# A head's normalisation and gating beside the opening of the next head, and a reordered start, in a hybrid decoder layer on one core

## The chip, the cores and the metric

The kernel runs on one core of a Trainium2 chip. The metric is device time in microseconds (us) of one execution. The engines are TensorE (PE in the profile, its weight loads PEld), VectorE (DVE), ScalarE (ACT), GpSimd (POOL) and SyncE (SP, which here only issues DMAs). A number such as L555 is a line of the kernel before.

## The reference

One layer, sequence 1024, width 2048, everything in fp32. A wide projection makes 15 column blocks of 512; four token mixers work on them (A, a gated convolution; B, a gated recurrence with 4 heads; C, differential attention with 4 heads; D, a chunked spatial gate); every mixer's output is multiplied by the silu of its own gate block; then an output projection, a layer norm and a gated addition of a second input.

```
h = x @ w_in                                   # (1024, 2048) @ (2048, 7680)
a_b,a_c,a_x, b_q,b_f,b_i, c_q,c_k,c_v, d_u,d_v, g_a,g_b,g_c,g_d = split(h, 15)
y_a = a_b * conv3(a_c * a_x)
# B, per head:  S_t = diag(f_t) S_{t-1} + (1-f_t) i_t^T ;  o_t = S_t^T q_t ;  rms norm
# C, per head:  (softmax(q1 k1) - lam * softmax(q2 k2)) v ;  rms norm
y_d = gelu(d_u) * (tril(W_s) LN(gelu(d_v)) + b)
y = concat(y_a*silu(g_a), y_b*silu(g_b), y_c*silu(g_c), y_d*silu(g_d)) @ w_out
x = layer_norm(ALPHA * x + y)
x = x + (p @ w_pe) * sigmoid(x @ w_pg)
```

## The kernel before

**The large products.** Each fp32 operand is split into a high part (a cast on ACT, L139) and the rest (a subtraction on DVE, L140), both in a reduced fp32 form; a product is then three runs of 128x512 matmuls (high by high, high by rest, rest by high), 24 matmuls in all for one 1024-long sum. The 2x2 block products of the input projection are done with seven products in place of eight (names P1, P6, P7, P4 in the first pass over 30 pairs of column blocks, N1, N4, A12 in the second). Sums of weight blocks (L262 to L271) and of x blocks (L312 to L320) are made on DVE. The first pass leaves its results in DRAM (`stash`), the second pass adds to them, and when a pair is complete its blocks are kept in DRAM (`h`) or, for gates, put through a silu and kept in `g_dram`.

**What runs beside the second pass.** Mixer work is written as Python generators, one for each head: `unit_c` and `mix_c` for a head of C, `unit_b` and `mix_b` for one of B, `values_d`, `norm_d` and `unit_d` for D. A completed pair appends its generator to `queue`. `step()` runs the first generator of the queue to its next `yield`; the second pass calls it after every second of the eight parts of a product, that is after every six matmuls. So the number of yields sets how many matmuls stand on PE between two pieces of mixer work. A head goes so: it issues the loads of its blocks from `h` (`back`, on POOL's queue), waits some yields, works, and ends with `rms` (a scale, a power on POOL, and the multiplication L548), seven yields, and `finish`: eight transposes on PE (`yt`, L555), two multiplications by the gate on DVE (L557), and a store to `y_dram` (L558, on SP's queue). Only then does the next generator begin, and the first thing that it does is to issue its loads.

**What sets the order.** Each engine takes its instructions in one order that a scheduler fixes when the kernel is built; work within `early()` is moved ahead of what stands before it in the code. Buffers are tiles with tags; a tag has one buffer unless the text says otherwise (`raw` 6, `wh` and `wl` 2 each, `E` 2, `pp` and `mx` 4 PSUM banks each). Work that writes a tile waits until the last user of the same buffer is done. So an engine that waits for a buffer or a load holds up what stands behind it, and `wh`, which PE needs for the next product, is often what stands behind it on ACT.

**The beginning.** SP loads one 512 KB block after another. `small_setup` (L98) makes small constants with some tiny DVE operations and one exponential on ACT (L103). The first pass then does P1 of pairs 0 to 3, P6 of pair 0, and so on, with the x sums S2 and S3 made in between.

**The end of the mixers.** After the last pair the loop `while len(queue) > 1: step()` and then the first output product (`tk`, L437) run the rest of the queue; the last head, B3, is in that product.

Of the kernel before, what the change touches and what calls it, by code (L numbers as in the profile page):

```python
# [16 lines left out]
P = 128  # L17
# [21 lines left out]
def trunk_kernel(  # L39
# [58 lines left out]
    def small_setup(pool):  # L98
        nc.gpsimd.dma_start(ident, tri[:, 0, :])
        nc.gpsimd.dma_start(chan_sb, chan)  # L100
        V.tensor_copy(lb_max, lb_raw)
        V.tensor_tensor(lb_e, lb_raw, lb_max, op=ALU.subtract)
        S.activation(lb_e, lb_e, AF.Exp)  # L103
        V.tensor_copy(one_lb, lb_e)
        V.reciprocal(one_lb, one_lb)
        V.tensor_tensor(lb_e, lb_e, one_lb, op=ALU.mult)
        V.tensor_copy(lb, lb_e)
        V.tensor_tensor(lb, lb, lb_e, op=ALU.subtract)
        V.tensor_scalar(one_lb, lb, -1.0, 1.0, op0=ALU.mult, op1=ALU.add)
        V.tensor_scalar_mul(da_g, chan_sb[:, 20:24], 1.0 - LAM_INIT)  # L110
        lamw = pool.tile([P, 4, 64], F32, tag="sm", bufs=4, name="lamw")
        nc.gpsimd.dma_start(lamw, lam_in.broadcast_to([P, 4, 64]))
        lamp = pool.tile([P, 2, 64], F32, tag="sm", bufs=4, name="lamp")
        V.tensor_tensor(lamp, lamw[:, 0::2, :], lamw[:, 1::2, :], op=ALU.mult)
        V.tensor_reduce(lamt[:, 0:2], lamp, axis=AX.X, op=ALU.add)
        S.activation(lamt[:, 2:4], lamt[:, 0:2], AF.Exp)
        V.tensor_tensor(lamt[:, 5:6], lamt[:, 3:4], lamt[:, 2:3], op=ALU.subtract)
        V.tensor_scalar_add(neg_lam, lamt[:, 5:6], -LAM_INIT)

    queue = []

    def step():
        while queue:
            if next(queue[0], queue) is not queue:
                return
            queue.pop(0)

    def drain():  # L130
        while queue:
            step()

    early = lambda: tc.high_priority(offset=4000)
# [70 lines left out]
    with tc.tile_pool(name="first", bufs=1) as first:  # L205
# [69 lines left out]
        def first_product(what, g, w=None):  # L275
            w = w or first_w(what, g)
            if what == "P1":
                chain[g] = pp.tile([P, H], F32, tag="pp", name=f"a{g}")
            ps = chain[g]
            products(ps, w, xs[{"P1": "A11", "P6": "S2", "P7": "S3", "P4": "A22"}[what]], what == "P1", True)  # L280
            if what in ("P1", "P7"):
                evs[g] = epool.tile([P, 2, H], F32, tag="e", name=f"ev{g}")

            S.copy(evs[g][:, {"P1": 0, "P6": 1, "P7": 1, "P4": 0}[what], :], ps)
            if what in ("P6", "P4"):
                i = 0 if what == "P6" else 1
                nc.scalar.dma_start(stash[g][:, i : i + 3 : 2, :], evs[g])
# [7 lines left out]
        for w in ("A11", "S2", "S3"):  # L295
            xs[w] = tuple([xa(f"{w}{i}{g}") for g in range(2)] for i in "hl")
        split_x = lambda w, t, q: split(t, pair(xs[w][0], q), pair(xs[w][1], q))
        with early():
            for q in range(4):
                nc.sync.dma_start(pair(r11, q), x_blk(1, 1, q))  # L300
                split_x("A11", pair(r11, q), q)
                if q == 0:
                    w_first = first_w("P1", 0)
        first_product("P1", 0, w_first)
        for g in (1, 2, 3):
            first_product("P1", g)
        with early():
            for q in range(4):
                nc.sync.dma_start(pair(r21, q), x_blk(2, 1, q))
                r22.append(sm(f"r22{q}"))  # L310
                nc.sync.dma_start(r22[q], x_blk(2, 2, q))
                V.tensor_tensor(pair(r21, q), pair(r21, q), r22[q], op=ALU.subtract)  # L312
                V.tensor_tensor(pair(r21, q), pair(r21, q), pair(r11, q), op=ALU.subtract)
                split_x("S2", pair(r21, q), q)
        for g in (2, 3):
            b[g].pop("11")
        first_product("P6", 0)
        with early():
            for q in range(4):
# [9 lines left out]
                split_x("A22", r22[q], q)  # L329
        first_product("P7", 1)  # L330
        first_product("P4", 0)
        first_product("P6", 2)
        first_product("P4", 1)
        first_product("P6", 3)
        first_product("P7", 2)
        first_product("P1", 4)
        first_product("P4", 2)
        first_product("P7", 3)
        first_product("P6", 4)
        first_product("P4", 3)  # L340
        small_setup(first)
        queue.extend([x_sums(q) for q in range(4)] + [w_sums(*HALVES[0], kk) for kk in range(8)])
        for g in range(5, NG):
            first_product("P1", g)
            step()
            if g == NG - 1:
                x_build("N1")
            first_product("P7", g - 1)
            first_product("P6", g)
            if g == NG - 1:  # L350
                x_build("A12")
            first_product("P4", g - 1)
# [112 lines left out]
    with tc.tile_pool(name="work", bufs=1) as work:  # L465
# [125 lines left out]
        def unit_b(j):  # L591
            k, f, qt, lw = wt("k1"), back(B_F, j, wt("l1")), back(B_Q, j, wt("q1")), wtE()
            iv = back(B_I, j, wtE())
            for _ in range(4):
                yield
            S.activation(k, f, AF.Sigmoid, scale=-1.0)
            S.activation(f, f, AF.Sigmoid)
            S.activation(k, k, AF.Copy, scale=one_lb[:, j : j + 1])
            V.tensor_scalar(f, f, one_lb[:, j : j + 1], lb[:, j : j + 1], op0=ALU.mult, op1=ALU.add)
            V.tensor_scalar_max(lw, f, SPLIT)  # L600
            V.tensor_scalar(f, f, F_FLOOR, SPLIT, op0=ALU.max, op1=ALU.min)
            S.activation(lw, lw, AF.Ln)
            S.activation(f, f, AF.Ln, scale=1.0 / SPLIT)
            V.tensor_tensor(f, f, lw, op=ALU.add)
            yield
            vtok = turned(wt("vt"), iv)
            yield
            yield from mix_b(j, k, f, qt, vtok)

        def mix_b(j, kt, lt, qt, vtok):  # L610
            at = ch(wt("a1"))
            G.memset(at, 0.0)

            near = wt("near", (P, 8, 32))
            G.memset(near, 0.0)

# [59 lines left out]
            pair_ = factors(LEVELS[0])  # L676
            yield
            yield
            for li, m in enumerate(LEVELS):
                ahead = factors(LEVELS[li + 1]) if li + 1 < len(LEVELS) else None  # L680
                yield
                gram(li, m, *pair_)
                pair_ = ahead
                if li + 1 < len(LEVELS):
                    yield
                    yield
# [8 lines left out]
            yield  # L695
            ktok = ch(wtV())
            transpose_to(ktok, ch(kt))
            o = ch(wtE())
            yield
            state = None  # L700
            ss = small.tile([P, 8], F32, tag="ss", name="ss")
            for b in range(2):
# [25 lines left out]
                S.copy(o[:, 4 * b : 4 * b + 4, :], pso)  # L728
                for c in range(4):
                    square(ss, 4 * b + c, pso[:, c, :])  # L730
            gt = gate_back("v1", 4 + j)
            rms(o, ss)
            for _ in range(7):
                yield
            finish(o, hg_g(j), gt, wt("o"), 4 + j)

        def unit_c(j):
            kraw, vraw, qraw = back(C_K, j, wt("o")), back(C_V, j, wtE()), back(C_Q, j, wtE())  # L740
            for _ in range(4):
                yield
            kh = [wt(t, dt=F32R) for t in ("l1", "q1")]
            kl = [wt(t, dt=F32R) for t in ("k1", "v1")]
            for mp in range(2):
                own = slice(64 * mp, 64 * mp + 64)
                oth = slice(64 - 64 * mp, 128 - 64 * mp)
                src, hi = kraw[own, :], kh[mp][own, :]
                S.copy(hi, src)
                S.copy(kh[mp][oth, :], src)  # L750
                V.tensor_tensor(kl[mp][own, :], src, hi.bitcast(F32), op=ALU.subtract)
                S.copy(kl[mp][oth, :], kl[mp][own, :].bitcast(F32))
            yield
            vtok = turned(wt("vt"), vraw)
            yield
            qs = [wt(t, dt=F32R) for t in ("a1", "x1")]
            for mp in range(2):
                own = slice(64 * mp, 64 * mp + 64)
                oth = slice(64 - 64 * mp, 128 - 64 * mp)
                src, hi = qraw[own, :], qs[mp][own, :]  # L760
                S.copy(hi, src)
                V.tensor_tensor(qs[mp][oth, :], src, hi.bitcast(F32), op=ALU.subtract)
            yield
            yield
            yield
            yield from mix_c(j, kh, kl, qs, vtok)

        def mix_c(j, kh, kl, qs, vtok):
# [58 lines left out]
            for i in range(NCH):  # L827
# [6 lines left out]
                last = (i, turn(i, a_t), rc)  # L834
                if i >= 4:
                    yield
            yield
            values(*last)
            gt = gate_back("l1", j)
            rms(o, ss)  # L840
            for _ in range(7):
                yield
            finish(o, da_g[:, j : j + 1], gt, gt, 8 + j)

        vd = []

# [401 lines left out]
```

## Time and profile before

| | before |
|---|---|
| median of 3 runs | 2127.43 us (2127.39 to 2134.34) |
| the profiled execution | 2130.79 us, span 2129.0 us |
| mean granted TensorE clock | 0.985 of full speed |
| PE busy | 2034.2 us, 96% of the span |
| DVE busy | 1358.8 us, 64% |
| ACT busy | 876.6 us, 41% |
| POOL busy | 150.1 us, 7% |
| DMA | 443.69 MB, 208 GB/s over the span |

PE is busy nearly always, so the time is close to the sum of its matmuls; what is not matmul is in the waits of PE, each of which has a line in the views of waits and of the timeline (idle time in square brackets, with what ended it). A wait of PE that is long can also be followed by a stretch in which the granted clock is half: the column PEclk of a stretch tells it (1.00 is 2.4 GHz throughout, a mean below it says what part of the stretch was at 1.2 GHz).

### The profile page before, as it was taken

What the parts mean: (1) busy time and instruction counts of PE and PEld (TensorE: products, weight loads), DVE (VectorE), ACT (ScalarE), POOL (GpSimd) and SP (SyncE); (2) the same over time, 40 slices, a digit from 0 to 9 for tenths busy, and PEclk for the clock granted to TensorE, in tenths of its full rate; (3) what the DMA queues carried; (4) which work ended last, traced back from release to release, by engine and by line L of the source; (5) the groups of instructions that cost most, each with busy time, mean ns of one, the idle gap of its engine ahead of it and who ended that gap; (6) DMA issues with size and microseconds to landing.
All of it is one profiled execution on the core that took longest, in us unless ns stands there. A gap on an engine that the chain in (4) does not pass through costs nothing. (4 is left out here: it accounts for less than half of the span.)

```text
span 2129.0 us, 27564 instructions
## 1 busy us (share of the span) xinstructions
PE 2034.2 (96%) x10732; PEld 1659.9 (78%) x10732; DVE 1358.8 (64%) x1679; ACT 876.6 (41%) x1304; POOL 150.1 (7%) x228
## 2 busy tenths in 40 slices
PE   7999999999999989999899999998999999999989
PEld 5788888778787777778678778777878888888867
DVE  7644545545455445557557678786767999355785
ACT  4322222222223446662665556563222345433432
POOL 0000001101100000010000000000121100000000
PEclk8999999999999999999999999999999999999999
DMA  6756767767768755467554554687687643423563
GB/s 238 240 192 225 261 230 251 278 241 248 268 236 287 257 170 177 130 208 250 181 165 135 197 190 159 209 309 245 231 300 254 223 168 119 138 92 107 191 200 133
DMA packets 169763, 443.69 MB, mean 208 GB/s; under 512 B 14432, under 2 KB 14704, under 8 KB 168352
## 3 DMA queue, kind: packets, MB, share of 16 engines
q1 hardware_dynamic: 120928, 292.80, 42.1%
q0 software_dynamic: 28064, 101.93, 13.4%
q10 hardware_dynamic: 20640, 47.19, 5.7%
q8 instruction: 84, 1.38, 0.3%
q14 instruction: 47, 0.39, 0.1%
HBM read 310.80 MB, written 131.07 MB: 208 GB/s over the span
## 5 line engine op out<-in xcount | busy, mean ns | idle before, releaser
L139 ACT CAST wh<-b 128x1024 fp32r<-128x1024 f32 x180 | 189.0, 1051 | 520.5 <-PE a L188 351.8
L437 PE MATMUL tk<-th,ah 128*128 128x512 f32 x832 | 326.8, 396 | 4.9 <-ACT ah L139 2.3
L437 PE MATMUL tk<-th,al 128*128 128x512 f32 x832 | 325.4, 391 | 5.2 <-DVE al L140 5.2
L437 PE MATMUL tk<-tl,ah 128*128 128x512 f32 x832 | 321.7, 392 | 2.3 <-DVE tl L140 2.3
L140 DVE TENSOR_TENSOR wl<-b,wh 128x1024 fp32r<-128x1024 f32 x180 | 219.9, 1222 | 161.5 <-ACT wh L139 161.2
L437 PEld LDWEIGHTS tk<-th,al 128*128 128x128 f32 x832 | 156.8, 188 | 39.3 <-DVE al L140 7.8
L437 PEld LDWEIGHTS tk<-th,ah 128*128 128x128 f32 x832 | 156.4, 188 | 39.7 <-ACT ah L139 3.7
L437 PEld LDWEIGHTS tk<-tl,ah 128*128 128x128 f32 x832 | 156.4, 188 | 36.5 <-DVE tl L140 3.8
L139 ACT CAST th<-t 128x1024 fp32r<-128x1024 f32 x64 | 67.4, 1054 | 201.3 <-PE tk L437 180.1
L262 DVE TENSOR_TENSOR b<-b,b 128x1024 f32<-128x1024 f32 x30 | 36.8, 1225 | 160.1 <-DMA b<-in_w_in_dram 160.1
L140 DVE TENSOR_TENSOR tl<-t,th 128x1024 fp32r<-128x1024 f32 x64 | 78.0, 1223 | 56.9 <-ACT th L139 56.7
L188 PE MATMUL a<-A22h,wl 128*128 128x512 f32 x240 | 95.4, 398 | 10.2 <-DVE wl L140 10.2
L188 PE MATMUL b<-N1h,wh 128*128 128x512 f32 x240 | 96.9, 404 | 7.2 <-ACT wh L139 7.2
L188 PE MATMUL a<-S2h,wh 128*128 128x512 f32 x240 | 95.8, 399 | 8.3 <-ACT wh L139 5.3
L139 ACT CAST th<-b 128x1024 fp32r<-128x1024 f32 x48 | 50.5, 1052 | 125.8 <-PE tk L437 98.9
L188 PE MATMUL a<-S2h,wl 128*128 128x512 f32 x240 | 95.8, 399 | 3.6 <-DVE wl L140 3.6
L188 PE MATMUL c<-A12h,wh 128*128 128x512 f32 x240 | 97.1, 404 | 2.1 <-ACT wh L139 2.1
L188 PE MATMUL a<-S2l,wh 128*128 128x512 f32 x240 | 95.5, 398 | 3.4 <-DVE S2l L140 3.4
L188 PE MATMUL b<-N4h,wh 128*128 128x512 f32 x240 | 96.8, 403 | 0.6 <-ACT th L139 0.6
L188 PE MATMUL b<-N4h,wl 128*128 128x512 f32 x240 | 97.0, 404 | 0.0
L188 PE MATMUL b<-N1h,wl 128*128 128x512 f32 x240 | 95.8, 399 | 1.0 <-DVE wl L140 1.0
L188 PE MATMUL c<-A12h,wl 128*128 128x512 f32 x240 | 96.2, 401 | 0.5 <-DVE wl L140 0.5
(334 smaller groups left out, 4547.0 us busy)
## 6 DMA issues: line engine op xcount, KB each, us to landing
b<-in_w_in_dram SPq DMA_DIRECT2D x182, 512.0 KB, 4.7
stash<-ev ACTq DMA_DIRECT2D x60, 512.0 KB, 4.2
e<-stash SPq DMA_DIRECT2D x60, 512.0 KB, 4.9
s<-in_w_out_dram POOLq DMA_DIRECT2D x32, 512.0 KB, 7.4
ot<-s POOLq DMA_DIRECT2D x32, 512.0 KB, 5.9
h<-e SPq DMA_DIRECT2D x32, 512.0 KB, 4.9
t<-ot SPq DMA_DIRECT2D x32, 512.0 KB, 4.7
t<-b ACTq DMA_DIRECT2D x30, 512.0 KB, 4.1
```

What stands on the lines that cost most here:

```text
L139: S.copy(hi, raw)
L140: V.tensor_tensor(lo, raw, hi.bitcast(F32), op=ALU.subtract)
L188: T.matmul(ps, lhsT=w_[:, c], rhs=x_[k // 4][:, k % 4, :], start=(start and k == 0 and i3 == 0), stop=(k == 7 and i3 == 2), skip_group_che ...
L262: V.tensor_tensor(b22, b22, b12, op=ALU.add)
L437: T.matmul(ps[nn][m], lhsT=l[:, kk % 2, t], rhs=w[:, wi, :], start=(not cont and kk == 0 and i3 == 0), stop=(kk == 7 and i3 == 2), skip_gr ...
```

## The change

There are three parts. First, the ends of heads. `finish` is no longer part of the generator: it goes on a list `later`, and `step()` runs it when it has been called eight times more, while the queue goes on with the next head. `open_next()` lets the next head issue its loads before the present one is done. For this some tiles move: the gate is read back into `W` in place of `l1` or `v1` and the product is written over it; the output of a B head lies in `o` in place of `E`; the keys of a C head are loaded into `a1` in place of `o`, and its queries ahead of its values. Second, some yields are added: in `unit_c` the opening has 5 in place of 4, 3 stand between the query split and the value transposes and 4 behind these; in `unit_b` 5 in place of 4, and one more ahead of the first `gram`. Third, the beginning: SP's loads are written in the order in which they are used, five P1 products stand ahead of P6 of pair 0 in place of four (the fifth accumulates in a bank of `mx`), the list of products up to pair 5 is written out anew, and the tiny operations of `small_setup` are held behind those products, not at the start.

```diff
 def small_setup(pool):
     ...
-        V.tensor_copy(lb_max, lb_raw)
+        tc.keep_in_program_order(V.tensor_copy(lb_max, lb_raw))
     ...
-        V.tensor_scalar_mul(da_g, chan_sb[:, 20:24], 1.0 - LAM_INIT)
+        tc.keep_in_program_order(V.tensor_scalar_mul(da_g, chan_sb[:, 20:24], 1.0 - LAM_INIT))
...
-    queue = []
+    queue, later = [], []
     def step():
+        for todo in list(later):
+            todo[0] -= 1
+            if todo[0] == 0:
+                later.remove(todo)
+                todo[1]()
         while queue:
...
+    def open_next():
+        if len(queue) > 1:
+            next(queue[1])
     def drain():
-        while queue:
+        while queue or later:
             step()
...
+                pool, tag = (mx, "mx") if g == LEAD - 1 else (pp, "pp")
+                chain[g] = pool.tile([P, H], F32, tag=tag, name=f"a{g}")
...
+        LEAD = 5
+        with early():
+            load_x = lambda t, r, c, q: nc.sync.dma_start(t, x_blk(r, c, q))
+            for q in range(4):
+                load_x(pair(r11, q), 1, 1, q)
+                if q == 0:
+                    b[0] = {"11": w_raw(0, 1, 1)}
+                    w_first = w_split(b[0]["11"])
+                split_x("A11", pair(r11, q), q)
+            b[1] = {"11": w_raw(1, 1, 1)}
+            r22.extend(sm(f"r22{q}") for q in range(4))
+            for q in range(4):
+                load_x(pair(r21, q), 2, 1, q)
+                load_x(r22[q], 2, 2, q)
+                if q == 1:
+                    b[2] = {"11": w_raw(2, 1, 1)}
+            for g in range(3, LEAD):
+                b[g] = {"11": w_raw(g, 1, 1)}
+        first_product("P1", 0, w_first)
+        for g in range(1, LEAD):
+            with early():
+                w = w_split(b[g]["11"])
+                if g > 1:
+                    b[g].pop("11")
+            first_product("P1", g, w)
...
-        first_product("P6", 2)
     ...
-        first_product("P4", 3)
+        queue.extend([x_sums(q) for q in range(4)] + [w_sums(*HALVES[0], kk) for kk in range(8)])
+        for what, g in (
+            ("P6", 2), ("P4", 1), ("P6", 3), ("P7", 2), ("P6", 4), ("P4", 2),
+            ("P7", 3), ("P1", 5), ("P4", 3), ("P7", 4), ("P6", 5), ("P4", 4),
+        ):
+            first_product(what, g)
+            if what == "P1":
+                step()
...
 def unit_b(j):
-            for _ in range(4):
+            for _ in range(5):
...
 def mix_b(j, kt, lt, qt, vtok):
+            turns[0] = 0
     ...
             pair_ = factors(LEVELS[0])
             yield
             yield
+            yield
     ...
-            o = ch(wtE())
+            o = ch(wt("o"))
     ...
-            gt = gate_back("v1", 4 + j)
+            open_next()
+            gt = gate_back("W", 4 + j)
             rms(o, ss)
-            for _ in range(7):
-                yield
-            finish(o, hg_g(j), gt, wt("o"), 4 + j)
+            later.append([8, lambda: finish(o, hg_g(j), gt, gt, 4 + j)])
...
 def unit_c(j):
-            kraw, vraw, qraw = back(C_K, j, wt("o")), back(C_V, j, wtE()), back(C_Q, j, wtE())
-            for _ in range(4):
+            kraw, qraw, vraw = back(C_K, j, wt("a1")), back(C_Q, j, wtE()), back(C_V, j, wtE())
+            for _ in range(5):
                 yield
...
-            vtok = turned(wt("vt"), vraw)
-            yield
             qs = [wt(t, dt=F32R) for t in ("a1", "x1")]
...
-            yield
-            yield
-            yield
+            for _ in range(3):
+                yield
+            vtok = turned(wt("vt"), vraw)
+            for _ in range(4):
+                yield
...
 def mix_c(j, kh, kl, qs, vtok):
...
+            open_next()
             yield
             values(*last)
-            gt = gate_back("l1", j)
+            gt = gate_back("W", j)
             rms(o, ss)
-            for _ in range(7):
-                yield
-            finish(o, da_g[:, j : j + 1], gt, gt, 8 + j)
+            later.append([8, lambda: finish(o, da_g[:, j : j + 1], gt, gt, 8 + j)])
```

**The start, on ACT.** These are ACT's first rows (A11h and S2h are casts of x, wh of a weight block, ev a copy of a finished product out of PSUM, t_0 the DMA that stores a sum of weight blocks), before:

```order
L103 ACTIVATE lbt<-lbt 128x4
L139 CAST wh<-b_0_461 128x1024
L139 CAST A11h_446<-r_442 128x1024 x2
L139 CAST A11h_447<-r_443 128x1024 x2
L139 CAST wh<-b_1_503 128x1024
L139 CAST wh<-b_2_536 128x1024
L284 COPY ev_501<-a_476 128x512
L139 CAST wh<-b_3_569 128x1024
```

and now:

```order
L151 CAST A11h_446<-r_442 128x1024
L151 CAST wh<-b_0_459 128x1024
L151 CAST A11h_446<-r_442 128x1024
L151 CAST A11h_447<-r_443 128x1024 x2
L151 CAST wh<-b_1_476 128x1024
L297 COPY ev_521<-a_496 128x512
L151 CAST S2h_450<-r_444 128x1024
L297 COPY ev_552<-a_527 128x512
L151 CAST wh<-b_2_486 128x1024
```

The exponential is gone from the head of the queue and the first cast of x leads; the weight cast for the third product, which stood ahead of every copy, stands behind the copies of the first two products and a cast of S2.

**From the first C head to the second, on PE.** `yt` are the transposes of the first head's end, `tr` the value transposes and `sc` the first scores of the second head; the rows between are the matmuls of the large products. Before:

```order
L188 MATMUL c_6072<-A12h_4676,wl 128x512
L555 MATMUL yt<-ident,o 128x128 x8
L535 MATMUL tr<-ident,E 128x128 x8
L188 MATMUL c_6072<-A12h_4676,wh 128x512
...
L188 MATMUL b_5889<-N4l_4758,wh 128x512
L783 MATMUL sc<-l_5872,a_5921 128x128
L783 MATMUL sc<-q_5873,x_5922 128x128
L188 MATMUL b_5889<-N4h_4756,wl 128x512
```

and now:

```order
L200 MATMUL c_6074<-A12h_4678,wh 128x512
L578 MATMUL yt<-ident,o 128x128 x8
L558 MATMUL tr<-ident,E 128x128 x8
L807 MATMUL sc<-l_5843,a_5861 128x128
L808 MATMUL sc<-k_5845,a_5861 128x128
L810 MATMUL sc<-causal,own 128x128
L807 MATMUL sc<-q_5844,x_5862 128x128
```

Before, 35 matmuls of the large products stood between `tr` and the first `sc`; now there are none, while `yt` itself stands 7 such matmuls later.

**The last head of B, on PE.** `hgo` is the last matmul of the head that waits for its state, `yt` its end, `tk` the output product. Before:

```order
L727 MATMUL hgo<-state,q_10886 128x128 x4
L437 MATMUL tk_11271<-th,ah 128x512
L437 MATMUL tk_11271<-th,al 128x512
L437 MATMUL tk_11271<-tl,ah 128x512
...
L437 MATMUL tk_11274<-tl,ah 128x512
L555 MATMUL yt<-ident,E 128x128 x8
```

and now:

```order
L460 MATMUL tk_11239<-th,ah 128x512
L460 MATMUL tk_11239<-th,al 128x512
L460 MATMUL tk_11239<-tl,ah 128x512
L752 MATMUL hgo<-state,q_10885 128x128 x4
L578 MATMUL yt<-ident,o 128x128 x8
L460 MATMUL tk_11623<-th,ah 128x512
```

The twelve `tk` matmuls that stood between `hgo` and `yt` now stand ahead of `hgo`.

## Rows read from the trace of the kernel before

**Rows 1.** The page, first part: busy us, share of the span and instructions by engine.

```profile
PE 2034.2 (96%) x10732; PEld 1659.9 (78%) x10732; DVE 1358.8 (64%) x1679; ACT 876.6 (41%) x1304; POOL 150.1 (7%) x228
```

**Rows 2.** Stretches: length, busy (instructions) of PE, PEld, DVE, ACT, POOL; PEclk, DMA share, GB/s.

```profile
4.00:18.00 14.00, 11.42 (x87) 9.74 (x86) 8.21 (x15) 5.88 (x7) 0.00 (x0) 0.88 1.04 386
42.00:60.00 18.00, 9.94 (x24) 6.45 (x25) 18.00 (x17) 9.06 (x10) 0.00 (x0) 0.62 0.33 111
106.00:373.00 267.00, 267.00 (x1180) 221.12 (x1179) 136.06 (x117) 75.21 (x98) 21.99 (x34) 1.00 0.69 232
848.00:874.00 26.00, 20.11 (x80) 16.29 (x79) 12.14 (x18) 13.74 (x17) 0.59 (x1) 0.80 0.48 142
1015.00:1030.00 15.00, 8.91 (x30) 6.56 (x29) 9.08 (x15) 11.56 (x16) 0.00 (x0) 0.66 0.51 170
1091.00:1110.00 19.00, 14.50 (x73) 11.27 (x72) 11.97 (x15) 12.87 (x14) 1.69 (x2) 1.00 0.47 141
1260.00:1268.00 8.00, 5.37 (x26) 4.41 (x25) 5.46 (x7) 4.35 (x6) 1.65 (x1) 0.79 0.83 267
```

**Rows 3.** PE timeline, first pass: start, length, instruction, [idle before <-releaser].

```profile
7.62 1.19 PE L89 MATMUL ps_idle<-idle 128*128 128x128 bf16 x15
...
10.28 0.50 PE L188 MATMUL a<-A11h,wh 128*128 128x512 f32 x1 [1.47 <-ACT A11h L139]
...
53.91 0.79 PE L188 MATMUL a<-S2h,wh 128*128 128x512 f32 x1 [5.33 <-ACT wh L139]
```

**Rows 4.** PE timeline, second pass and the last head, at its longer waits.

```profile
756.34 0.80 PE L188 MATMUL b<-N1h,wh 128*128 128x512 f32 x1 [4.35 <-ACT wh L139]
...
850.88 0.33 PE L555 MATMUL yt<-ident,o 128*128 128x128 f32 x1 [2.25 <-DVE o L548]
...
866.09 0.47 PE L783 MATMUL sc<-l,a 128*128 128x128 f32 x1 [3.63 <-ACT l L750]
...
945.83 0.33 PE L857 MATMUL tr<-ident,E 128*128 128x128 f32 x1 [4.27 <-DVE l L557]
...
1018.41 0.66 PE L188 MATMUL c<-A12h,wh 128*128 128x512 f32 x1 [1.79 <-ACT wh L139]
...
1023.80 0.45 PE L783 MATMUL sc<-l,a 128*128 128x128 f32 x1 [4.30 <-DVE a L762]
...
1104.87 0.33 PE L783 MATMUL sc<-l,a 128*128 128x128 f32 x1 [2.86 <-ACT l L750]
...
1456.76 0.30 PE L555 MATMUL yt<-ident,E 128*128 128x128 f32 x1 [2.69 <-DVE E L548]
```

**Rows 5.** ACT timeline, same columns.

```profile
8.14 0.21 ACT L103 ACTIVATE lbt<-lbt 128x4 f32<-128x4 f32 x1 [5.91 <-DVE lbt L102]
...
753.10 1.04 ACT L761 CAST a<-E 64x1024 fp32r<-64x1024 f32 x1 [11.13 <-DMA E<-h]
...
1013.03 1.05 ACT L749 CAST l<-o 64x1024 fp32r<-64x1024 f32 x1 [7.30 <-DMA o<-h]
...
1451.34 0.59 ACT L728 COPY E<-hgo 128x512 f32<-128x512 f32 x1 [1.28 <-PE hgo L727]
```

**Rows 6.** DVE timeline, same columns.

```profile
944.41 0.69 DVE L871 TENSOR_TENSOR vt<-vt,tri 128x512 f32<-128x512 f32 x1 [4.88 <-DMA vt<-in_sg_wT_dram]
```

**Rows 7.** DMA issues: queue, count, KB each, median us from issue to landing.

```profile
b<-in_w_in_dram SPq DMA_DIRECT2D x182, 512.0 KB, 4.7
...
t<-b ACTq DMA_DIRECT2D x30, 512.0 KB, 4.1
...
y_dram<-l SPq DMA_DIRECT2D x4, 512.0 KB, 5.0
```

**Rows 8.** Waits of PE summed: line, releaser, total us, times, longest us.

```profile
PE yt L555 <- DVE E L548: 5.7, 3, 2.7
...
PE yt L555 <- DVE o L548: 5.7, 4, 2.3
...
PE gram L639 <- DVE v L664: 3.3, 3, 1.4
```

More of the change, by code (lines that the diff above doesn't have):

```diff
@@ L277, in first_product @@
             if what == "P1":
-                chain[g] = pp.tile([P, H], F32, tag="pp", name=f"a{g}")
+                pool, tag = (mx, "mx") if g == LEAD - 1 else (pp, "pp")
+                chain[g] = pool.tile([P, H], F32, tag=tag, name=f"a{g}")
             ps = chain[g]
@@ L297, in trunk_kernel @@
         split_x = lambda w, t, q: split(t, pair(xs[w][0], q), pair(xs[w][1], q))
+        LEAD = 5
[23 more added lines that the diff above has]
+            first_product("P1", g, w)
         with early():
             for q in range(4):
[L300 to L311, printed above, removed]
                 V.tensor_tensor(pair(r21, q), pair(r21, q), r22[q], op=ALU.subtract)
@@ L314, in trunk_kernel @@
                 split_x("S2", pair(r21, q), q)
-        for g in (2, 3):
-            b[g].pop("11")
         first_product("P6", 0)
@@ L331, in trunk_kernel @@
         first_product("P4", 0)
-        first_product("P6", 2)
[L333 to L339, printed above, removed]
-        first_product("P4", 3)
+        queue.extend([x_sums(q) for q in range(4)] + [w_sums(*HALVES[0], kk) for kk in range(8)])
[6 more added lines that the diff above has]
+                step()
         small_setup(first)
-        queue.extend([x_sums(q) for q in range(4)] + [w_sums(*HALVES[0], kk) for kk in range(8)])
-        for g in range(5, NG):
+        for g in range(LEAD + 1, NG):
             first_product("P1", g)
```

## The prediction, made before the changed kernel was run

> **What bounds the kernel now.** First the page's busy times: PE is busy for 96% of the span, every other engine far less [rows 1], so only what shortens PE's waits, or raises its clock, shortens the time. Then the stretches: in 106 to 373 us PE is busy throughout at full clock, 1180 matmuls in 267 us, 0.226 us each, with DVE half idle [rows 2]; there is nothing to gain there. A product of 24 matmuls takes 5.43 us by it, and a step of the queue (six matmuls) 1.36 us. Last the waits of PE, in order of time. Those that the change can touch lie at the start [rows 3], and where one head ends and the next opens [rows 4, 8]. A wait costs more than itself where the clock falls behind it: 848 to 874 us has a granted clock of 0.80 and 20.11 us of PE work, so some 0.20 x 20.11 = 4.0 us went to matmuls at 1.2 GHz; 1015 to 1030 gives 0.34 x 8.91 = 3.0 us in the same way, 42 to 60 gives 0.38 x 9.94 = 3.8, 1260 to 1268 gives 0.21 x 5.37 = 1.1, while 1091 to 1110, with waits too, shows 1.00 [rows 2]. These figures are estimates, since a mean clock says nothing of which part of the stretch was idle.
>
> The sum is made against the profiled execution, 2130.79 us (span 2129.0 and 1.79 around it). The median of the runs is 3.4 us below that, 0.16%.
>
> **The start.** Before, ACT's queue is held until 8.14 us by the exponential of the small constants, which waits for DVE [rows 5]; A11h stands behind it, and the first product begins at 10.28, 1.47 us after the idle matmuls have ended [rows 3]. With the exponential gone and x ahead, the cast of the first x block follows its load, and I place the first product right behind the idle matmuls, at 7.62 + 1.19 = 8.8 us. But that is not what the stage ends on. Loads come at 386 GB/s from 4 to 18 us [rows 2], 1.36 us for 512 KB, and DVE is busy for all of 42 to 60 us [rows 2]; PE then stands 5.33 us until 53.91 for the `wh` of P6 of pair 1 [rows 3]. In the new order that `wh` needs pair 1's block 22, whose raw buffer is free when the sum t_0 has been stored (about 36.9 us when ACT comes to it, 4.1 for the store), then 4.7 us for the load [rows 7], so 45.7, and then its sums and the split behind other DVE work of 1.2 us an operation: 53 to 54 us, as before. What changes is that a fifth P1 has been done by then. One product is 5.4 us; the new waits that I see, for the weights of the third and fourth P1 (their casts stand behind copies of finished products on ACT, as the order ahead shows for the third), lie in time that PE would otherwise spend idle before P6 of pair 1. So 5.4, less 0.4 for the load slots that P6 of pair 4 now waits for: **-5.0**. Bounds: if the chain to that `wh` also shortens by the 3 us of a new wait no longer needed, -8; if it comes a product later and another stretch like 42 to 60 (3.8 us) falls in, +3.
>
> The page "DMA: Bandwidth & Descriptors" of the Trainium skill gives under Specifications about 358 GB/s as what the memory yields to one core; the trace shows 386 over 14 us, so the measurement decides. By the page each of some twelve loads would come 0.1 us later than before's spacing says, and P6 of pair 1 would start about 1 us later.
>
> The small DVE operations moved behind the first products cost nothing: DVE is busy for 136 of 267 us where they now stand [rows 2]. Without that cover they would be twelve operations at the 0.21 us of their exponential [rows 5], 2.5 us.
>
> **First to second C head.** The wait of 2.25 us for the end's multiplication and that of 3.63 us for the split of the keys [rows 4], with 4.0 us of clock: 9.9 us. The next head's loads are issued before the first head's last values, its keys are split while the norm is computed, and the two waits fall together, since `yt`, `tr` and `sc` stand in one place on PE with seven more matmuls ahead (7 x 0.226 = 1.6 us). What is late next is that same multiplication, still behind the query split on DVE: 2.25 - 1.6 = 0.6 us, and about 1.9 for the scores' first values. 9.9 - 2.5: **-7.4**. Ends: -9.9 if nothing remains, -2 if all the operands arrive as late as before and only the clock gains.
>
> **Second C head to D.** PE stood 4.27 us because the gate product L557 was late on DVE [rows 4], behind L871, which itself waited 4.88 us for a load [rows 6]. `finish` now stands ahead of that row. But the transposes of D's first block now come right behind the head's last values, and need a load that was only just issued; I leave 1.3 us for it: **-3.0** (ends -4.3 and 0).
>
> **The opening of the third C head.** ACT waits 7.30 us for the keys, which are loaded into `o`, late, since the D branch's `o` is in use [rows 5]; behind it stand `wh` for a large product (1.79 us on PE) and the queries, for which PE waits 4.30 more [rows 4]; with the clock's 3.0 that is 9.1. With the keys in `a1`, the queries second and seven steps in place of three ahead of the scores (4 x 1.36 = 5.4 us more), 4.30 is covered and most of the rest; 2 us are left: **-7.1** (ends -9.1 and -3).
>
> **Third to fourth C head, fourth to the first of B.** The one had 2.86 us for the scores [rows 4] and, with the transposes' part of the 5.7 us in four waits [rows 8], about 4.4; the other about 1.5. By the first boundary's rule a half goes: **-3.5** together (ends -6 and 0).
>
> **B's heads.** The ends waited 5.7 us in three places, 2.69 of it at the last head, so 3.0 here, the grams 3.3 [rows 8], the clock 1.1. One more step ahead of the grams is 1.36 us, against 1.4 for the longest gram wait; the ends' squares and norm have the next head's opening beside them. **-4.0** (ends -7.4 and 0).
>
> **The last head** has no next one to stand beside. The order shows the twelve `tk` matmuls now ahead of the last `hgo`. From the copy of `hgo` at 1451.34 [rows 5] to `yt` at 1456.76 [rows 4] are 5.4 us, of which 2.69 were idle and the rest was those twelve. The wait becomes 5.4, 2.7 more, and behind a wait of about that length at 53.91 the clock is low [rows 2, 3]; a third of that 3.8 is 1.3. **+4.0** (ends +2.7 and +6.5).
>
> **The gate tile.** `finish` now writes its result over the gate in `W` and stores it: 5.0 us [rows 7] until the next head can use `W`, which C needs for its first transposed probabilities and B for its second factors. From `yt` the store lands 1.6 + 5.0 = 6.6 us later; the next head's first use stands about 22 matmuls behind, 5 us and some scores. So it is nearly even: 0.4 us at each of seven changes, **+3.0** (ends 0 and the rival below). Behind that copy on ACT stands the next `wh`.
>
> Sum: -5.0 -7.4 -3.0 -7.1 -3.5 -4.0 +4.0 +3.0 = -23.0, and 2130.79 - 23.0 = 2107.8; as the median stands a little lower, I say **2107 us**.
>
> **The rivals.**
>
> *The store of W decides* (slower). If an ACT copy waits for `W`, all that is behind it waits. What such a wait makes of PE is seen where ACT stood until 753.10 for a load and PE then waited 4.35 us for `wh` [rows 4, 5]. At that price in all seven changes, and 1.1 us of clock each as at 1260 [rows 2], it takes 7 x 5.4 = 38 us in place of the 3.0 in the sum: 2107 + 35 = 2142. It needs more than 3.7 us at each change ((23.0 + 3.0) / 7) to make the kernel slower than the profiled execution. For it: 6.6 us against 5. Against it: `wh` has two buffers, so a large product of 5.4 us is covered, and for B the user is DVE, behind which less hangs. The Trainium skill, "TensorE: Matmul & The Clock Gate", under "Wait — 56ns, not 53.3ns?", says that ACT and DVE work strictly first in, first out; the row at 753.10 agrees, and by that rule this rival stands or falls with the store alone.
>
> *The waits only move.* The loads into `E` still come late, since two buffers hold everything; the yields only put `sc` behind matmuls that then lack their weights; the start's fifth P1 is eaten by waits for the third and fourth. Then a third of the 30.0 us of gains is left, 10, against 7 of losses: 2128 by the profile, 2119 to 2134. For it: the waits of ACT at 753 and 1013 are for loads [rows 5], and of the loads into `E` the change makes none earlier than the head before it allows.
>
> *All boundaries close.* Every gain at its far end, -8 -9.9 -4.3 -9.1 -6 -7.4 = -44.7, with the losses at +2.7: 2089; half way to it from the sum, 2096.
>
> *The start does not do what it says*: P6 of pair 1 later, so that the fifth product ahead buys nothing. The sum without its 5: 2112, still faster.
>
> **How the numbers follow.** About 0.5% (10.6 us) is what a measurement of this kernel can tell from no change, so 2116.8 and 2138 are the borders around the median. My sum, with its terms half right, 2099 to 2115: 0.52. All boundaries close: 0.10. The start without gain: 0.08. The waits only move: 0.22, of which 0.03 lies on the faster side. W decides: 0.08, of which 0.01 stays within. Faster: 0.52 + 0.10 + 0.08 + 0.03 = 0.73 less 0.03 for the upper end of the sum, 0.70; same 0.23; slower 0.07. The range leaves out a tenth on either side: 2093 to 2129.
>
> **What would show it.** In the new profile: the first product at 8.8 us and P6 of pair 1 near 54 to 56 with a wait of over 5 us still there; no wait over 1.5 us at the first scores of the second, third and fourth C head, and a granted clock near 1.00 in those stretches; the tail's `yt` behind a wait of about 5.4 us. It is wrong if ACT copies of the transposed probabilities wait for a DMA of `y_dram`, or if the removed waits reappear at `wh` or `wl` within the same 50 us.

## The result, and the profile after

| | before | changed |
|---|---|---|
| median, first measurement | 2128.31 us (4 runs, 2127.39 to 2134.34) | 2102.20 us (4 runs, 2094.97 to 2103.97) |
| ratio, with its 95% interval | | 0.988 [0.9854, 0.9906] |
| second measurement | 2124.44 us (11 runs) | 2107.41 us (6 runs), 0.9915 [0.9898, 0.9932] |
| profiled execution | 2130.79 us, span 2129.0 | 2100.59 us, span 2098.8 |
| PE busy, mean clock | 2034.2 us, 0.985 | 2026.4 us, 0.989 |

Faster by about 1%: 2107 was forecast. To see where the 30.2 us between the two profiled executions come from, every PE matmul is counted with the median time between two starts of its shape at full clock, and the two kernels are compared at equal counts: the lead is how much earlier the changed kernel stands there. The last column is the profiled execution of the second measurement (2107.93 us), compared with the same execution of the kernel before.

| stage | lead at its end | gained | forecast | gained, second measurement |
|---|---|---|---|---|
| start, to about 106 us | 8.7 | 8.7 | 5.0 | 6.0 |
| rest of the first pass | 9.7 | 1.0 | 0 | 2.7 |
| opening of the first C head | 12.0 | 2.3 | 0 | 0.9 |
| first to second C head | 20.5 | 8.5 | 7.4 | 8.0 |
| second C head to D | 22.1 | 1.6 | 3.0 | -1.0 |
| opening of the third C head | 24.8 | 2.7 | 7.1 | 3.1 |
| third to fourth C head, to B | 28.4 | 3.6 | 3.5 | 3.1 |
| heads of B | 36.1 | 7.7 | 4.0 | 7.5 |
| last head | 31.4 | -4.7 | -4.0 | -5.9 |
| W, anywhere | | 0 to be seen | -3.0 | 0 to be seen |
| rest | 30.2 | -1.2 | 0 | -1.5 |

A stage of a single execution is known only to a few us: the start's lead lies between 4.4 and 8.7 us, 6.0 in the middle, in the nine profiled executions that have this start (this kernel's two, and those of the experiments that leave the start as it is here). The 8.7 above is the far end. In the rest of the first pass even the heads-only kernel of the first experiment, whose code there is that of the kernel before, gained 2.9 us.

PE at the start of the changed kernel (start, length, instruction, idle time before it and its releaser), which answers to [rows 3]:

```profile
7.80 1.46 PE L89 MATMUL ps_idle<-idle 128*128 128x128 bf16 x19
9.07 0.47 PE L200 MATMUL a<-A11h,wh 128*128 128x512 f32 x1
...
21.86 0.50 PE L200 MATMUL a<-A11h,wh 128*128 128x512 f32 x1 [1.62 <-ACT wh L151]
...
51.65 0.80 PE L200 MATMUL a<-S2h,wh 128*128 128x512 f32 x1 [3.70 <-ACT wh L151]
```

The first product follows the idle matmuls without a wait; the new wait for the third P1's weights is there (21.86); P6 of pair 1 starts at 51.65 and not at 53 to 54.

PE further on, answering to [rows 4]:

```profile
744.87 0.50 PE L200 MATMUL b<-N1h,wh 128*128 128x512 f32 x1 [2.60 <-ACT wh L151]
...
838.75 0.44 PE L578 MATMUL yt<-ident,o 128*128 128x128 f32 x2 [0.50 <-DVE o L571]
848.25 0.49 PE L845 MATMUL pv<-vt,W 128*128 128x128 f32 x2 [0.63 <-ACT W L839]
919.29 0.95 PE L880 MATMUL tr<-ident,E 128*128 128x128 f32 x7 [1.56 <-DMA E<-h]
926.17 1.06 PE L880 MATMUL tr<-ident,E 128*128 128x128 f32 x8 [2.38 <-DMA E<-h]
980.03 0.50 PE L200 MATMUL c<-A12h,wh 128*128 128x512 f32 x1 [2.89 <-ACT wh L151]
...
1069.49 0.77 PE L578 MATMUL yt<-ident,o 128*128 128x128 f32 x5 [1.19 <-DVE o L571]
...
1420.11 1.30 PE L578 MATMUL yt<-ident,o 128*128 128x128 f32 x5 [6.21 <-DVE o L571]
...
1443.90 0.80 PE L460 MATMUL tk<-th,al 128*128 128x512 f32 x1 [3.35 <-DVE al L152]
```

No first score of a C head waits for its operands any more, where 3.63, 4.30 and 2.86 us stood. At D the wait is for loads now, and the last head waits 6.21 in place of 2.69.

Stretches (length, busy time and instructions of PE, PEld, DVE, ACT and POOL; granted clock, DMA share, GB/s), answering to [rows 2]:

```profile
836.00:862.00 26.00, 24.87 (x130) 19.42 (x130) 15.74 (x33) 17.81 (x34) 0.00 (x0) 1.00 0.55 182
978.00:993.00 15.00, 12.45 (x47) 9.85 (x48) 5.85 (x7) 5.01 (x5) 1.05 (x2) 0.89 0.75 240
1415.00:1430.00 15.00, 9.89 (x36) 8.29 (x37) 3.89 (x6) 2.40 (x10) 3.17 (x3) 0.77 0.42 140
1440.00:1455.00 15.00, 11.31 (x38) 8.44 (x37) 13.06 (x16) 3.15 (x3) 0.00 (x0) 0.77 0.80 285
```

Between the first two C heads the granted clock is 1.00 where it was 0.80, at the third 0.89 where it was 0.66; at the last head it is 0.77 twice.

ACT at the three places where it waits for a DMA that the forecast spoke of, answering to [rows 5]:

```profile
741.64 1.05 ACT L783 CAST a<-E 64x1024 fp32r<-64x1024 f32 x1 [9.38 <-DMA E<-h]
...
847.93 0.27 ACT L839 COPY W<-att 128x128 f32<-128x128 f32 x1 [0.96 <-DMA y_dram<-W]
...
971.48 1.04 ACT L773 CAST q<-a 64x1024 fp32r<-64x1024 f32 x1 [6.21 <-DMA a<-h]
```

The second row is the only ACT wait for the store of `W`: 0.96 us, of which 0.63 reach PE. The third says that the third C head's keys still came late.

### The profile page after: what moved, and what is told of

Its sections match the earlier page's. It is cut to its first block, busy times and chain, and to the rows that moved or that the text cites. A ratio compares the mean times of both kernels' runs of the same rounds, so it can differ in the third digit from the quotient of the medians.

```text
span 2098.8 us, 27539 instructions
## 1 busy us (share of the span) xinstructions
PE 2026.4 (97%) x10732; PEld 1657.8 (79%) x10732; DVE 1360.3 (65%) x1679; ACT 878.1 (42%) x1307; POOL 151.2 (7%) x228
## 5 line engine op out<-in xcount | busy, mean ns | idle before, releaser
L200 PE MATMUL a<-A11h,wh 128*128 128x512 f32 x240 | 94.2, 393 | 1.6 <-ACT wh L151 1.6
L200 PE MATMUL a<-A11h,wl 128*128 128x512 f32 x240 | 94.4, 393 | 1.3 <-DVE wl L152 1.3
```

Source lines behind the costliest of these rows:

```text
L200: T.matmul(ps, lhsT=w_[:, c], rhs=x_[k // 4][:, k % 4, :], start=(start and k == 0 and i3 == 0), stop=(k == 7 and i3 == 2), skip_group_che ...
```

## The experiments

**The start alone, and the heads alone.** The kernel before with the change's start; the changed kernel with the start of before (LEAD, the order of loads, the list of products and `small_setup` as one piece).

> The kernel before with only the new start (order of loads, five leading P1, small constants later); the heads as before. Theory 1 (the two halves are independent and the start's lead is kept): the lead over the kernel before is some 8.7 us by the 360th matmul of the large products, as in the changed kernel, and stays to the end: 2128 - 9 = 2119 us. Theory 2 (the start's lead is given back where the first pass waits for loads and copies): under 4 us at the end, 2124 us or more.

> The changed kernel with the start of the kernel before; only the heads are changed. Theory 1: the rest of the 30 us of the profiled executions, 21 us: 2107 us, with the first 680 us as before. Theory 2 (part of the heads' gain exists only with the new start): under 15 us, 2113 us or more.

Measured: the start alone 2117.63 against 2124.05 us, 0.9964 [0.9949, 0.9978]; the heads alone 2109.55, 0.9928 [0.9905, 0.9951]. In the traces the start's lead is 6.8 us after the start and never given back, and that of the heads-only kernel is 21 us, of which 3.1 were there before the first C head; in time they gave 6.4 and 14.5. So theory 1 holds for the start, and for the heads the traces speak for it, while by the times the heads lie just under the 15 of theory 2; their interval reaches from 10 to 20 us, so the times alone do not decide. 0.9964 x 0.9928 = 0.9892 lies between the two measurements of the whole change (0.988 and 0.9915): the halves add up, and nothing shows that one needs the other.

**Four leading products.**

```diff
-        LEAD = 5
+        LEAD = 4
```

(and the old list of products behind them, with the sums' queue begun where it was)

> The changed kernel with four leading P1 products in place of five and the old list of products behind them; the new order of loads and the late small constants stay. Theory 1 (the fifth product is worth its own length, because P6 of pair 1 waits for the same chain either way): the first P6 matmul of pair 1 starts near 51.7 us as in the changed kernel, its wait grows from 3.7 to about 9 us, and the lead over the kernel before falls from 8.7 to about 3.3 us. Theory 2 (the order of the loads carries the gain): P6 of pair 1 starts some 5 us earlier and the lead stays above 7 us.

PE of that kernel:

```profile
39.27 0.50 PE L200 MATMUL a<-S2h,wh 128*128 128x512 f32 x1 [2.64 <-ACT wh L151]
...
51.87 0.50 PE L200 MATMUL a<-S2h,wh 128*128 128x512 f32 x1 [2.37 <-ACT wh L151]
...
74.23 0.55 PE L200 MATMUL a<-A22h,wl 128*128 128x512 f32 x1 [4.71 <-DVE wl L152]
```

P6 of pair 1 starts where it did in the changed kernel (51.87 against 51.65), with a product less done: theory 1. Its wait did not grow to 9 us, since PE already waited at P6 of pair 0 (39.27) and again at 74.23. The lead is 0.6 us where 3.3 was expected, 3.8 to 8.1 below the nine executions with five leading products, whose middle is the length of one product away. One run, 2108.21 against 2126.12.

**The constants.** `small_setup`'s operations free to stand at the start again, in the changed kernel; and, alone, pinned behind the first products in the kernel before:

```diff
-        tc.keep_in_program_order(V.tensor_copy(lb_max, lb_raw))
+        V.tensor_copy(lb_max, lb_raw)
...
-        tc.keep_in_program_order(V.tensor_scalar_mul(da_g, chan_sb[:, 20:24], 1.0 - LAM_INIT))
+        V.tensor_scalar_mul(da_g, chan_sb[:, 20:24], 1.0 - LAM_INIT)
```

(the second of the two kernels has it the other way round)

> The changed kernel with the small constants' DVE operations and exponential free to stand at the start again. Theory 1 (the first product's start is not what the stage ends on): the first product comes 1 to 1.5 us later, and the lead after the start falls by under 0.5 us. Theory 2: all of it is carried, the lead falls by 1 us or more.

> The kernel before, and of the change only that the small constants' operations stand behind the first products. Theory 1 (the constants alone hold up ACT and DVE until 8 to 9.5 us, and what they hold up is carried on by the weight casts that stand behind copies of finished products): the first product starts near 9 us, the low clock at 12 us is gone, and the lead over the kernel before after the start is 2 to 5 us. Theory 2 (they cost only together with the new order of loads, since in the old order the stage ends on DVE from 25 us on): under 1 us of lead after the start, time as before.

DVE of the first of the two, and then PE:

```profile
7.75 0.17 DVE L101 COPY lbt<-chan_sb 128x4 f32<-128x4 f32 x1 [6.78 <-DMA chan_sb<-in_chan_dram]
...
9.40 0.17 DVE L109 TENSOR_SCALAR lbt<-lbt 128x4 f32<-128x4 f32 x1
9.48 1.23 DVE L151 TENSOR_TENSOR A11l<-r,A11h 128x1024 fp32r<-128x1024 f32 x1
```

```profile
10.29 0.50 PE L199 MATMUL a<-A11h,wh 128*128 128x512 f32 x1 [1.48 <-ACT wh L150]
...
56.72 0.80 PE L199 MATMUL a<-S2h,wh 128*128 128x512 f32 x1 [3.99 <-ACT wh L150]
```

Theory 2 holds: the lead after the start is 3.2 us, less than in any of the nine executions with the constants behind the first products (4.4 to 8.7). DVE's first subtraction stands at 9.48 behind the wait for a small load, where the changed kernel had it at 5.61; P6 of pair 1 comes at 56.72, 5.1 us later than there, though the first product was only 1.2 later. In the nine it comes at 51.7 to 53.3, so the constants cost 3.4 to 5.1 us at P6 of pair 1. (One run, 2106.43 us.) Alone in the kernel before, the edit starts the first product at 8.19 us and gives 3.1 us of lead after the start, as theory 1 says, but no time that can be told: 2128.70 against 2128.24, 0.9992 [0.9973, 1.0011].

**The order of queries and values.**

```diff
-            kraw, qraw, vraw = back(C_K, j, wt("a1")), back(C_Q, j, wtE()), back(C_V, j, wtE())
+            kraw, vraw, qraw = back(C_K, j, wt("a1")), back(C_V, j, wtE()), back(C_Q, j, wtE())
```

> The changed kernel with the C heads' values loaded ahead of their queries again. Theory 1 (the first C head's gain of 2.3 us, which was not forecast, comes from the order of these two loads): ACT's wait for the queries grows from 9.4 to over 11 us, PE's 2.60 us wait for wh goes back to about 4.3, and some 2 to 3 us of lead are lost there; at the later C heads, whose loads are issued a head's end earlier, little. Theory 2 (it comes from the extra step in the opening): nothing moves there.

```profile
743.58 1.04 ACT L783 CAST a<-E 64x1024 fp32r<-64x1024 f32 x1 [11.50 <-DMA E<-h]
```

```profile
746.81 0.79 PE L200 MATMUL b<-N1h,wh 128*128 128x512 f32 x1 [4.72 <-ACT wh L151]
```

Theory 1: ACT and then PE of that kernel wait as before (PE's wait is 1.95 to 3.09 us in ten other traces with the queries first), and 3.5 us of lead go at this place; up to the end of the C heads no more than 1.7 follow. One run, 2102.80 us.

**The third head's keys in W.**

```diff
-            kraw, qraw, vraw = back(C_K, j, wt("a1")), ...
+            kraw, qraw, vraw = back(C_K, j, wt("W" if j == 2 else "a1")), ...
```

> The changed kernel, with the third C head's keys loaded into W in place of a1. Theory 1 (a1 is still held by the third D block, so the load is issued only when that is done, 962.7 us in the trace): the load is issued some 9 us earlier, ACT's wait of 6.21 us for it is gone, and with it PE's 2.89 and 0.53 us and the low clock behind them: some 4 to 5 us, 2097 us. Theory 2 (the load would be late anyway, since the DMA engines are busy there): ACT still waits over 4 us for it and the time stays at 2102.

POOL's issues in it, a store on SP between them, and ACT:

```profile
956.25 0.59 POOL L550 DMA_DIRECT2D a<-h  x1 [15.00 <-DVE E L930]
963.16 0.53 POOL L550 DMA_DIRECT2D W<-h  x1 [6.33 <-issue]
```

```profile
956.58 0.34 SPq L547 DMA_DIRECT2D h<-e  x1
```

```profile
971.66 1.04 ACT L773 CAST q<-W 64x1024 fp32r<-64x1024 f32 x1 [9.73 <-DMA W<-h]
...
973.79 1.05 ACT L151 CAST wh<-b 128x1024 fp32r<-128x1024 f32 x1
```

The same POOL issues, and that weight cast, in the changed kernel:

```profile
952.30 0.59 POOL L550 DMA_DIRECT2D a<-h  x1 [14.98 <-DVE E L930]
962.70 0.53 POOL L550 DMA_DIRECT2D a<-h  x1 [9.81 <-DVE E L930]
```

```profile
964.22 1.05 ACT L151 CAST wh<-b 128x1024 fp32r<-128x1024 f32 x1 [6.20 <-PE c L200]
```

Theory 1 falls as to the gain: 2100.25 us, 0.9874 [0.9844, 0.9905], no difference from the changed kernel. The times 962.70 and 963.16 can't be set side by side, because this execution stands some 4 us behind the other here. Counted from the load of the third D block's `u` in the row above it, the keys' load comes after 6.9 us in place of 10.4, so 3.5 us earlier and not 9. The profile names no releaser for it; it is issued 0.5 us after the store of 956.58 has landed (6.1 us), which is probably the store of these very keys, but that is not shown. It then takes 8.4 us. The edit also changed ACT's order: the weight cast that stood ahead of the keys at 964.22 stands behind them at 973.79. So this run doesn't isolate what `a1` costs; PE's wait there is 2.27 us against 2.89.

**The end 12 steps behind the norm.**

```diff
-            later.append([8, ...
+            later.append([12, ...
```

> The changed kernel with a head's end run 12 steps behind its norm in place of 8, so four steps (5.4 us) later. Theory 1 (the end's waits are for the multiplication, and W has slack): the waits of PE at yt of 0.5, 1.19, 1.24 and 1.77 us go, ACT's one wait for the store of W stays near 1 us, and the kernel gains 3 to 4 us. Theory 2 (the store of W decides, the rival forecast as slower): ACT waits for the store of W at two or more C heads, 4 us or more each, PE waits behind it for pv or wh, and the kernel loses 5 us or more.

Measured: 2106.17 us (one run). The four waits at `yt` are gone, but PE waits elsewhere: 1.00 and 0.86 us for value loads into `E`, 2.20 for a factor of B, whose multiplication waited for `W`. ACT, then DVE:

```profile
1085.81 0.27 ACT L839 COPY W<-att 128x128 f32<-128x128 f32 x1 [2.71 <-DMA y_dram<-W]
```

```profile
1172.23 0.69 DVE L694 TENSOR_TENSOR W<-k,E 128x512 f32<-128x512 f32 x1 [2.42 <-DMA y_dram<-W]
```

Neither theory: the store of `W` begins to show, at one C head and one head of B, but it does not decide. At eight steps it is out of the way.

**The last head at the old steps.**

```diff
-            for _ in range(5):
+            for _ in range(5 if j < 3 else 4):
...
-            yield
-            yield
-            yield
+            for _ in range(3 if j < 3 else 2):
+                yield
```

> The changed kernel, with the last head of B alone at the old number of steps (4 and 2 in place of 5 and 3), so that its transposes stand behind twelve matmuls again. Theory 1 (the last head's 6.21 us wait, against 2.69 before, comes from those twelve matmuls being ahead of the last state product): the wait is about 2.7 us, the low clock behind it is gone, and the time is some 5 us below the changed kernel's 2102: 2097 us. Theory 2 (the wait comes from the longer chain of the gate tile W): the wait stays above 5 us and the time at 2102.

> The changed kernel once more, beside the next two on the same chip. Both theories: 1.0 to 1.5% below the kernel before, as first measured (0.988). In the trace, if the stages are what I take them for: 8 to 9 us of lead after the start, some 8 between the first and the second C head, 7 or more lost at the last B head; the stretch between the second C head and D anywhere from 0 to 3, since the loads of D's blocks came at different times in the runs so far.

> The last head of B at the old number of steps, once more beside the changed kernel. Theory 1 (the wait at the last head is on the path to the end): 3 to 5 us below the changed kernel on the same chip, 0.2%, and the wait at the last yt 2.7 us. Theory 2 (what is gained there is given back where the output product then waits for x blocks, z, 4.08 us in the first run of this kernel): within 1 us of the changed kernel, with that z wait 1 to 2 us longer than in the changed kernel.

PE of its first run:

```profile
1420.08 1.25 PE L578 MATMUL yt<-ident,o 128*128 128x128 f32 x8 [2.70 <-DVE o L571]
...
1542.92 0.47 PE L460 MATMUL tk<-th,ah 128*128 128x512 f32 x1 [4.08 <-DVE z L1012]
```

The wait is 2.70 us again, and 4.9 us of lead come back at this place; 1.2 go at the wait for `z`. In time the first run shows nothing (2102.15), the second, beside the changed kernel on one chip, 2102.46 against 2107.41: 0.9891 [0.9872, 0.9910] against 0.9915 [0.9898, 0.9932]. The intervals overlap: the mechanism is shown; its worth in time was 5 us in the second pair and nothing in the first.

The changed kernel again was 0.85% below the kernel before, less than the 1.0 to 1.5 expected. Of the stages named, the first to the second C head came as expected (8.0), the start gave 6.0 in place of 8 to 9, and the second C head to D lost 1.0 where 0 to 3 were expected; at the last head 9.6 us are lost from the highest lead (34.0) on. PE at D in it:

```profile
929.64 0.66 PE L880 MATMUL tr<-ident,E 128*128 128x128 f32 x2 [3.68 <-DMA E<-h]
```

**D's third and fourth blocks later** (on top of the last edit):

```diff
             e = back(D_V, j, wtE())
-            for _ in range(4):
+            for _ in range(8 if j > 1 else 4):
                 yield
```

> As the kernel before this in the list, and the third and fourth D blocks wait eight steps in place of four between load and transposes. Theory 1 (the wait of 4 to 5 us at D's transposes and the low clock behind it come from those two loads, issued when a buffer of E is free and landing 7 to 8 us later): these waits fall under 1 us and the kernel gains 4 to 6 us there. Theory 2 (the wait is pushed on to the D units or the third C head, whose keys then come later): the lead at the end of the C heads is the same within 1 us.

The stretch of 900 to 1000 us, without this edit and then with it:

```profile
900.00:1000.00 100.00, 90.55 (x440) 74.19 (x440) 58.91 (x90) 37.62 (x59) 11.25 (x16) 0.93 0.68 233
```

```profile
900.00:1000.00 100.00, 95.00 (x486) 78.46 (x485) 66.35 (x97) 42.97 (x64) 11.78 (x17) 1.00 0.76 265
```

PE in the first, and then in the second:

```profile
928.23 1.09 PE L879 MATMUL tr<-ident,E 128*128 128x128 f32 x4 [4.05 <-DMA E<-h]
...
984.96 0.79 PE L200 MATMUL c<-A12h,wh 128*128 128x512 f32 x1 [3.87 <-ACT wh L151]
```

```profile
929.67 0.52 PE L879 MATMUL tr<-ident,E 128*128 128x128 f32 x3 [0.92 <-DMA E<-h]
...
988.81 0.50 PE L200 MATMUL b<-N4h,wh 128*128 128x512 f32 x1 [1.27 <-ACT wh L151]
...
1443.45 0.79 PE L460 MATMUL tk<-th,ah 128*128 128x512 f32 x1 [4.06 <-ACT ah L151]
```

Theory 1, and more: the wait at D's transposes falls from 4.05 to 0.92 us, that at the third C head from 3.87 to 1.27, and the clock stays at 1.00. By the end of the C heads 9 us of lead more than without it. Some 2.5 of these are left by 1550 us: B's heads and the output product wait longer in this trace (4.06 us for `ah` where the other has 1.30), and why is open. 2096.75 us, 0.9866 [0.9845, 0.9888]: the fastest of all. With the edit of the last head that it stands on it is 10.7 us below the changed kernel on the same chip, whose interval [0.9898, 0.9932] lies wholly above; this edit alone is the 5.7 us from 2102.46, where the intervals overlap.

## Why the prediction was right

The sum was -23.0 and the two measurements gave -26 and -17, the profiled pair -30.2. The mechanisms of the larger terms are those forecast, but several sizes were off and partly cancelled, so that the total came out near 2107 is in part luck. The execution of the second measurement gave 22.9, the sum almost to the figure: there D and the third C head fell short by 4.0 each and the last head cost 1.9 more, while B's heads gave 3.5 more than forecast, W cost 3.0 less, and the rest of the first pass with the first C head gave 3.6 that no term had. Of the signs named, P6 of pair 1 came sooner and behind 3.70 us, not over 5, and the clock at the third C head was 0.89. In "all boundaries close", half way from 2107 to 2089 is 2098, not 2096.

- *The start*, -5.0, was -8.7 in the first trace and 4.4 to 8.7 over nine, so the forecast is a little under their middle. The chain to P6 of pair 1 was the right one, and the fifth P1 is what it gives time for (four leading products: 0.6 us of lead). But I took 4.1 and 4.7 us for the store and the load in it, medians of the whole run [rows 7], and P6 came 2 us sooner. DMA issues of 36 to 52 us of the new trace, with the median from issue to landing last:

```profile
b<-in_w_in_dram SPq DMA_DIRECT2D x3, 512.0 KB, 3.9
t<-b ACTq DMA_DIRECT2D x2, 512.0 KB, 2.7
```

  And the constants, put at nothing since the work in their new place hides them, cost 3.4 to 5.1 us at P6 of pair 1 in their old one: I priced where they went, not what they had held up. The loads of 4 to 18 us came as fast as before (last column, GB/s), so the 358 GB/s of the Trainium skill, "DMA: Bandwidth & Descriptors" under Specifications, played no part:

```profile
4.00:18.00 14.00, 14.00 (x105) 12.47 (x104) 9.53 (x8) 6.88 (x7) 0.00 (x0) 1.00 1.05 387
```

- *The first C head*, 0, was -2.3: queries loaded ahead of values. The sum has no term for it; of the loads into `E` the prediction says only that none comes earlier than the head before it allows, and the first head has none before it.
- *First to second C head*, -7.4, was -8.5, with the clock's part as sized.
- *Second C head to D*, -3.0, was -1.6 here. In four other traces of the same code 4.2 to 4.7 us of waiting and a clock of 0.93 in 900 to 950 us stand there, and the stage loses about 1 us: the loads of the third and fourth D block took the place of the gate's wait. The step that failed is the 1.3 us left for D's loads.
- *The third C head's opening*, -7.1, was -2.7. The step that failed is "with the keys in `a1`": the third D block's `u` lies there, the load was issued at 962.7 and took 8.7 us, and ACT waited 6.21 us for it where it had waited 7.30. The 4.30 us at the scores went, but the wait for `wh` grew from 1.79 to 2.89. With the keys in W no time was gained. What helps is spacing D's blocks.
- *Third and fourth C head*, -3.5, was -3.6.
- *B's heads*, -4.0, were -7.7. PE's idle time in this stage fell from 9.2 to 5.1 us and 1.1 of clock went; the other 2 to 3 us are not traced to a wait.
- *The last head*, +4.0, was +4.7, with two terms that I had not counted. The kernel before waits there for `ah` and `al` at the output product's first steps (1.44 and 0.93 us); without these the lead first rises to 40.0. Then 8.6 go: the wait 6.21 for 5.4, a new one of 3.35 for `al` (4.80 in the second measurement's trace), and the low clock behind each.
- *W*, +3.0, was 0.63 us, though its stores took 6.3 us in the median and not 5.0. The rival that it decides is ruled out at eight steps; at twelve the store is seen. Where ACT did wait for a DMA, at 741.64 and 971.48, `wh` came late behind it; so the rule of the Trainium skill, "TensorE: Matmul & The Clock Gate", that ACT works strictly first in, first out (it stands there under "Architectural detail: the array is 16× 32×32, not 1× 128×128", and not under the heading that the prediction names) agrees with the trace, and only the wait that it needed was missing.

The rival that the waits only move is right for D, and in part for the third C head (`wh`) and the last head (`al`).

## What to carry to other kernels

Where one unit of work ends with a long chain on other engines, queue the next unit's opening ahead of that end, and look for the last unit, which has nothing to stand beside. Price an operation that is moved away by what stood behind it in its queue, at its old place, not by its own length. Size a DMA in a chain by the stretch in which it runs: in that of 36 to 52 us a store took 2.7 us against a median of 4.1, and the keys that were issued at 962.7 took 8.7.

## What the runs showed that was not expected

An edit of 3.1 us at the start of the kernel before left no time that could be told in ten runs. The same program's two profiled executions had 22.9 and 30.7 us of lead over the kernel before by 1720 us. Most of the difference lies at the start behind P6 of pair 1 (2.7 us), at the first C head's opening (1.4) and at D (2.6), and in each of these the execution with less lead has a lower clock (0.97 in 60 to 110 us, 0.88 in 736 to 765, 0.93 in 900 to 950) than the other (1.00, 0.94, 1.00). A wait is best read from a trace, the gain of a stage from several traces, and a total from several runs.
